# RWKV layer of a two-layer trunk: raw weight loads kept three ahead in another ring, and half of the output weight staged through three tiles

## The chip, the cores and the metric

One core of one Trainium2 chip runs the whole kernel in one launch. The metric is device time in microseconds (us), from a median of separate runs; lower is better. The engines are TensorE (PE for its matmuls, PEld for its weight loads), VectorE (DVE), ScalarE (ACT), GpSimd (POOL) and SyncE (SP), which in this kernel issues all transfers between DRAM and on-chip memory, in one order.

## What is computed

A sequence of 2048 tokens of width 1024 in float32 passes two layers. Each adds to x a normalised mixer of the normalised x. Layer 1 is gated linear attention. Layer 2, which the change touches, is RWKV-7 (cut from the reference):

```python
p = h @ w_in                                   # 2048 x 1024 @ 1024 x 4224
p = p + mu * (token_shift(p) - p)
r, k, v, gate, wd, ad = jnp.split(p, ...)
...
def step(S, inp):                              # over the 2048 tokens, 16 heads of 64
    r_t, w_t, k_t, v_t, kk_t, a_t = inp
    sa = jnp.einsum('bhvk,bhk->bhv', S, -kk_t)
    S = (S * w_t[:, :, None, :] + sa[..., None] * (kk_t * a_t)[:, :, None, :]
         + v_t[..., None] * k_t[:, :, None, :])
    y = jnp.einsum('bhvk,bhk->bhv', S, r_t)
    return S, y
...
return y.astype(h.dtype) @ w_out               # then: x + RMSNorm_post(this)
```

## The kernel before, in words

Layer 1 and its output projection fill the first 880 us or so. Layer 2 is the function `rwkv`. Tokens are cut in four quarters of 512, channels in eight blocks of 128 (two heads). A **step** handles one quarter of one block in chunks of 64 tokens; there are 32 steps of about 42.5 us, then the output projection. A step's own work (`step`) is projections into its tiles, the decay and rate `a` (ACT, L1219 to L1227), products of the form `TD` (POOL, L1233), the chunk matrices (`pA` on PE writes `ps_tp<-ra,bk`, then an elimination on DVE, L1419 and L1422, tiles `pp` and `L`), and the state chain (PE `ps_ch<-ve,BK`, ACT `ve<-ps_ch,cs`, L1601). One of its tiles is `ra`, a 128 x 1024 tile that holds alpha and r, from a ring of three buffers.

All matmuls that carry float32 precision use a high and a low part of each operand: a **block** is one 128-wide slice of a weight against 512 tokens, 8 slices of the inner size by 3 products (high by high, high by low, low by high), 24 matmuls of 128x512. A block needs its 1024 x 128 weight slice, 512 KB, in three tiles: raw (`ws`, ring of one buffer), high `wh` and low `wl` (rings of two).

- `fetch` (L951 to L961) takes the next entry of the list `blocks` and loads its raw slice into `ws` (SP, L960).
- `split` (L963 on) makes high and low. **Quick** blocks do it on ACT (cast, L139) and DVE (subtract, L140), in halves. The others do it on POOL: high in L989, low in L993, and the order in which POOL comes to these is fixed by the table described below.
- `keep` (L976 to L980) writes high and low of a new weight slice to DRAM, so that later quarters read them back (L999) and don't split again. So new slices are split only in the prologue and in steps 0 to 7.
- Then `fetch` is called for the following block.

Quick are the five blocks with step number 0 (`wa`, `kx`, `rx`, `vx`, and `sg`, the gate), and the last 16 blocks, which are the output projection. There the token slice `ys` of 512 KB takes the part of the weight slice.

The order of the list: four blocks of step 0 come ahead of all steps (the prologue; after it, the blocks of the next step are spread through each step as *filler*: 16 pieces, `f0` to `f15`, each a quarter of a block). Near the end eight blocks called `out` compute the product of the first 1024 tokens with the first half of the output weight `wo` (`outfirst`, L372) and write it to DRAM (`raw`). Then `outproj` (L380 to L446) runs: for each of the eight token blocks of half 0 it reads `raw` back into a `vx` tile, computes the product with wo's second half (24 matmuls into `ps_tp`), and finishes the rows (ACT squares L435, DVE L396 and L400, POOL L401, load of x L395, store L402). For each of the eight token blocks of half 1 both halves of wo are used (48 matmuls into `ps_pj` and `ps_tp`).

wo's halves (and the normalised input of later quarters) come in through `eighths` (L169 to L187): eight pieces of 128x512, each loaded into the one-buffer tile `qs` (SP, L177), cast on ACT into `R` (L180), subtracted on DVE (L184); a piece's subtraction calls `more`, which starts the next piece.

Order within an engine: in the steps PE, DVE, ACT and POOL run in an order fixed by a table (`PLACE`: each named event has a due time in steps). SP's order, and that of all engines outside the steps, is made by a scheduler, so the code below says which instructions exist and what they depend on, and the order views further down say where they stand.

Of the kernel before, what the change touches and what calls it, by code (L numbers as in the profile page):

```python
# [17 lines left out]
P = 128  # L18
# [5 lines left out]
TB = 512  # L24
# [26 lines left out]
class Trunk:  # L51
# [3 lines left out]
    def __init__(self, ctx, tc, ins, out):  # L55
# [12 lines left out]
                a=1, kkx=1, sq=1, y=1, AD=1, L=1, Tl=1, TD=1, TT=1, pp=1, wt=1, wa=1, xw=1, xa=1, us=1,   # L68
# [97 lines left out]

        return split

    def eighths(self, src, done, then):  # L169

        hi = self.t("R", NK, TB, dt=F32R)
        lo = self.t("R", NK, TB, dt=F32R)
        done.append((hi, lo))

        def load(k):
            st = self.t("qs", TB)
            self.nc.sync.dma_start(st, src[k * P:(k + 1) * P, :])  # L177

            def high():
                self.nc.scalar.copy(hi[:, k, :], st)  # L180
                self.put("part.low", low)

            def low():
                self.nc.vector.tensor_sub(lo[:, k, :], st, hi[:, k, :].bitcast(F32))  # L184
                then()

            self.put("part.high", high)  # L187
        return [lambda k=k: load(k) for k in range(NK)]
# [731 lines left out]
    def rwkv(self, g, out):  # L920
        nc, i = self.nc, self.i
        w, wo = i["rwkv_w_in"][0], i["rwkv_w_out"][0]
# [3 lines left out]
        hT, W, tiles, parts = [], [], {}, []  # L926

        keys, blocks = [], []
# [10 lines left out]
        for name, m in keys:  # L939
# [3 lines left out]
            blk = off[name] + (steps[m][1] if name != "wa" else 0)  # L943
            blocks.append((w[:, blk * P:(blk + 1) * P], NK, P, m == 0, blk))

        kept = {}
        blocks += [(self.yrows(1, half, j), NK, P, True, None) for half in range(NH) for j in range(8)]

        nxt, ready = SimpleNamespace(), []

        def fetch():  # L951
            nxt.raw = None
            if not blocks:
                return
            src, a, b, quick, blk = blocks.pop(0)
            if blk in kept:
                nxt.raw = None, quick, blk
                return
            st = self.t("ws", 1024)
            nc.sync.dma_start(st.rearrange("p (k c) -> p k c", k=a), src.rearrange("(k p) c -> p k c", p=P))  # L960
            nxt.raw = st, quick, blk  # L961

        def split(name):  # L963

            if nxt.raw is None:
                return
            st, quick, blk = nxt.raw
            pair = []
            ready.append(pair)

            def parts():
                hi, lo = (self.t(t, 1024, dt=F32R) for t in ("wh", "wl"))
                pair.extend(x.rearrange("p (k c) -> p k c", k=NK) for x in (hi, lo))
                return hi, lo

            def keep(hi, lo):  # L976
                if blk is not None:
                    kept[blk] = [self.dr.tile([P, 1024], F32, tag=f"w{j}_{blk}", name=f"w{j}_{blk}", bufs=1) for j in range(2)]
                    for d, x in zip(kept[blk], (hi, lo)):
                        nc.sync.dma_start(d, x.bitcast(F32))  # L980

            def high():
                hi, lo = parts()
                if quick:
                    self.split(st, hi, lo, True)
                    keep(hi, lo)
                    fetch()
                else:
                    nc.gpsimd.tensor_scalar(hi, st, 1.0, 0.0, op0=ALU.mult, op1=ALU.add)  # L989
                    self.put(name + ".low", lambda: low(hi, lo))  # L990

            def low(hi, lo):
                nc.gpsimd.tensor_sub(lo, st, hi.bitcast(F32))  # L993
                keep(hi, lo)
                fetch()

            if st is None:
                for x, d in zip(parts(), kept[blk]):
                    nc.sync.dma_start(x.bitcast(F32), d)  # L999
                fetch()  # L1000
            elif quick:
                high()
            else:
                self.put(name + ".high", high)

        def more():

            if parts and len(blocks) < 25:
                self.put("part", parts.pop(0))

        def take(name="out"):
            split(name)
            if parts and len(blocks) >= 25 and len(blocks) % self.EVERY == 0:
                self.put("part", parts.pop(0))
            return ready.pop(0)

        def stream():
            for name, m in keys:
                if name == "out":
                    yield from self.outfirst(m, take(name), W[0])  # L1020
                    continue
                half, hp, tb = steps[m]
                blk = off[name] + (hp if name != "wa" else 0)
                o = tiles[name, m] = self.t(name, TB)
                then = None
                if name == "wa":
                    res = tiles["x", m] = []
                    then = lambda o=o, res=res: self.lowrank(o, res)
                yield from self.projw(name, hT[m // NHP], take(name), blk, o, then)
                if name == "sg" and (m == 0 or hp == NHP - 1):  # L1030

                    q = m // NHP + 2 if m else 1
                    if q < NH * NTB:
                        parts.extend(self.eighths(self.h2[q], hT, more))
                    else:
                        ch = q - NH * NTB
                        parts.extend(self.eighths(wo[:, ch * TB:(ch + 1) * TB], W, more))
                        more()
            yield from self.outproj(take, W, g, self.x1, out, raw=self.raw)


# [2 lines left out]
        for m, t in enumerate(self.first):  # L1044
            k = slice(2 * m, 2 * m + 2)
# [9 lines left out]
        nc.gpsimd.memset(self.Ti, 0.0)  # L1055
        fetch()
        split("out")
        filler = stream()

        self.load_up(0)  # L1060
# [643 lines left out]
```

## Time and profile before

| | |
|---|---|
| runs of the kernel before | 2526.58, 2529.47 (median), 2530.96 us |
| the profiled execution | 2529.55 us; its span in the trace 2527.5 us |
| mean granted clock of TensorE | 0.988 of full speed |
| PE busy | 95% of the span, 20049 matmuls |
| ACT, DVE, POOL busy | 65%, 63%, 42% |
| DMA | 312.85 MB, 124 GB/s mean over the span |
| quick splits, L139 / L140 | 116 each, mean 608 / 721 ns |

How to read it. The time of the profiled execution is 2 us above its span and 0.08 us above the median of the runs. PE is busy nearly all the time, so what counts are the few places where PE waits or runs at a lower granted clock. In a row of the timeline, the square bracket behind an instruction is the idle time of its engine ahead of it and what ended that. In a row of windows the first number is the window's length, then come busy time and instruction count of PE, PEld, DVE, ACT and POOL, the granted clock (1.00 is full speed, 2.4 GHz; 0.50 is 1.2 GHz), the share of time that the 16 DMA engines were busy, and GB/s.

### The profile page before, as it was taken

To read this page: it belongs to the slowest core of one execution; us is meant where nothing else is said; L and a number is where in the kernel's file an instruction comes from. 1 tells how busy PE (TensorE), PEld (TensorE's weight loads), DVE (VectorE), ACT (ScalarE), POOL (GpSimd) and SP (SyncE) were. 2 spreads that over 40 slices of the span, in tenths; PEclk is the share of its full clock that TensorE was granted. 3 is DMA by queue.
4 is the path that set the end of the run, shared out by engine and by line. 5 is a ranking of instruction groups with operands and counts; after the bars stand their busy time and mean duration, and the time that the engine had idled before them with its cause. 6 is when DMAs were issued, how large, how long until landed. Compare 5 with 4: busy or idle time off the path is not lost.

```text
span 2527.5 us, 53044 instructions
## 1 busy us (share of the span) xinstructions
PE 2413.4 (95%) x20049; PEld 2015.0 (80%) x20049; DVE 1592.1 (63%) x3339; ACT 1645.6 (65%) x3890; POOL 1056.3 (42%) x1557
## 2 busy tenths in 40 slices
PE   7999999999999979999999999999999999999888
PEld 6988888898788857777778788787787878777667
DVE  6544776445643347878777776767677777774332
ACT  6534565444523336877888888788888888877421
POOL 3213422123355536766544443344433434344332
PEclk9999999999999989999999999999999999999999
DMA  4211343112546565444433333333333333323573
GB/s 147 84 51 51 110 124 97 47 51 82 177 141 222 168 207 164 147 145 145 143 112 131 123 118 112 123 123 115 126 109 114 112 122 124 118 76 97 164 222 110
DMA packets 251862, 312.85 MB, mean 124 GB/s; under 512 B 18745, under 2 KB 180184, under 8 KB 251608
## 3 DMA queue, kind: packets, MB, share of 16 engines
q1 hardware_dynamic: 251608, 309.47, 37.3%
q8 instruction: 159, 2.61, 0.4%
q14 instruction: 95, 0.78, 0.1%
HBM read 230.77 MB, written 78.64 MB: 122 GB/s over the span
## 4 chain that ended last, share of the span: by engine, by line
PE 37%; ACT 17%; DVE 4%; issue 3%; DMA 2%; POOL 1%; POOLq 0%; SPq 0%; ACTq 0%; DVEq 0%
PE ps_pj L103 20%; PE ps_tp L103 9%; PE ps_x L103 3%; ACT AD L1377 2%; PE ps_ch L103 2%; ACT ve L1601 2%; PE ps_y L103 1%; ACT ve L1322 1%; ACT ts L836 1%; ACT BK L1394 1%; DMA ws<-ys 1%; PE ps_tp L1561 1%; ACT y L1615 1%; ACT wt L1492 1%; DVE pp L1419 1%
## 5 line engine op out<-in xcount | busy, mean ns | idle before, releaser
L103 PE MATMUL ps_pj<-R,wh 128*128 128x512 f32 x3648 | 1174.6, 403 | 8.0 <-ACT wh L139 3.0
L103 PEld LDWEIGHTS ps_pj<-R,wh 128*128 128x128 f32 x3648 | 657.5, 190 | 136.3 <-ACT wh L139 3.9
L103 PE MATMUL ps_pj<-R,wl 128*128 128x512 f32 x1824 | 720.7, 395 | 11.6 <-POOL wl L993 8.3
L103 PEld LDWEIGHTS ps_pj<-R,wl 128*128 128x128 f32 x1824 | 344.8, 189 | 92.1 <-POOL wl L993 10.4
L1601 ACT ACTIVATE ve<-ps_ch,cs 64x64 f32<-64x64 f32 x448 | 137.3, 307 | 61.5 <-PE ps_ch L103 52.9
L1419 DVE TENSOR_TENSOR pp<-L 128x14 f32<-128x14 f32 (+6 forms) x448 | 168.3, 376 | 10.5
L103 PE MATMUL ps_tp<-R,wh 128*128 128x512 f32 x512 | 160.7, 394 | 13.1 <-ACT R L180 6.6
L139 ACT CAST wh<-ws 128x512 fp32r<-128x512 f32 (+2 forms) x116 | 64.9, 608 | 140.9 <-PE ps_pj L103 68.8
L1422 DVE TENSOR_TENSOR L<-L,pp 128x14 f32<-128x14 f32 (+6 forms) x448 | 136.9, 306 | 12.2
L140 DVE TENSOR_TENSOR wl<-ws,wh 128x512 fp32r<-128x512 f32 (+2 forms) x116 | 79.7, 721 | 91.1 <-ACT wh L139 91.1
L832 POOL TENSOR_SCALAR carr<-ts 128x1 f32<-128x1 f32 x132 | 32.6, 247 | 248.6 <-ACT ts L836 248.5
L1548 POOL TENSOR_SCALAR A<-ra 64x512 f32<-64x512 f32 x128 | 89.8, 701 | 103.6 <-PE ps_x L103 52.4
L308 POOL TENSOR_TENSOR s<-s,cc 128x1 f32<-128x1 f32 (+1 forms) x96 | 58.0, 605 | 170.4 <-DVE s L306 161.8
L103 PEld LDWEIGHTS ps_tp<-R,wh 128*128 128x128 f32 x512 | 96.5, 189 | 36.1 <-ACT wh L139 7.5
L103 PE MATMUL ps_ch<-ve,BK 128*128 128x128 f32 x512 | 109.2, 295 | 7.3 <-ACT ve L1601 7.1
L1377 ACT COPY AD<-A 32x128 f32<-32x128 f32 x256 | 104.9, 410 | 11.3 <-DVE A L1367 8.3
L103 PEld LDWEIGHTS ps_ch<-ve,BK 128*128 128x128 f32 x512 | 87.3, 189 | 29.9 <-ACT ve L1601 10.6
L836 ACT ACTIVATE ts<-ps_pj,prm 128x512 f32<-128x512 f32 x132 | 91.3, 691 | 21.3 <-PE ps_pj L103 12.8
L1367 DVE TENSOR_TENSOR A<-ps_tp,mask 128x512 f32<-128x512 f32 x128 | 82.4, 683 | 34.2 <-PE ps_tp L103 34.2
L103 PE MATMUL ps_tp<-R,wl 128*128 128x512 f32 x256 | 100.8, 394 | 0.0
L1580 DVE TENSOR_TENSOR BK<-ps_tp,BK 128x256 f32<-128x256 f32 x128 | 53.6, 419 | 68.6 <-PE ps_tp L103 68.4
L103 PE MATMUL ps_pj<-wh,R 128*128 128x256 f32 (+1 forms) x500 | 94.7, 287 | 0.0
(354 smaller groups left out, 5489.4 us busy)
## 6 DMA issues: line engine op xcount, KB each, us to landing
wh<-w SPq DMA_DIRECT2D x99, 512.0 KB, 3.3
wl<-w SPq DMA_DIRECT2D x99, 512.0 KB, 4.2
ws<-in_rwkv_w_in_dram SPq DMA_DIRECT2D x33, 512.0 KB, 4.7
w<-wh SPq DMA_DIRECT2D x33, 512.0 KB, 2.6
w<-wl SPq DMA_DIRECT2D x33, 512.0 KB, 3.1
Ti<-in_gla_w_in_dram SPq DMA_DIRECT2D x32, 512.0 KB, 3.9
ws<-in_gla_w_in_dram SPq DMA_DIRECT2D x32, 512.0 KB, 3.8
ws<-ys SPq DMA_DIRECT2D x32, 512.0 KB, 4.0
```

Source lines behind the costliest of these rows:

```text
L103: return self.nc.tensor.matmul(out, lhsT, rhs, start=start, stop=stop)
L139: self.nc.scalar.copy(hi[:, c], src[:, c])
L140: self.nc.vector.tensor_sub(lo[:, c], src[:, c], hi[:, c].bitcast(F32))
L308: nc.gpsimd.tensor_tensor(r[:, 0:w], u[:, 0:w], self.nhalf.broadcast_to([P, w]), op=ALU.pow)
L836: nc.scalar.activation(ts[:, 1:TB + 1], pp, AF.Copy, scale=self.v["mu"][:, blk:blk + 1])
L1367: dve.tensor_mul(T.A[cg][:, :, :, h, :], V(T.pA[cg][h]), V(self.mask.unsqueeze(1).broadcast_to([P, 4, 2 * C])))
L1377: act.copy(T.AD[q, :, :, cg * 4:cg * 4 + 4].rearrange("p t u c -> p c u t"), T.A[cg][q, :, 0, h, 32 * b:32 * b + 32].rearrange("p c (u t) ...
L1419: dve.tensor_mul(T.u, T.M[:, s + 1:16, s:s + 1].broadcast_to([P, m, s]), T.M[:, s:s + 1, 0:s].broadcast_to([P, m, s]))
L1422: dve.tensor_add(T.M[:, s + 1:16, 0:s], T.M[:, s + 1:16, 0:s], T.u)
L1548: pool.tensor_scalar(T.A[cg][H[h], :, :, h, :], T.ra[H[h], cg * 4:cg * 4 + 4, :].rearrange("p c (b t) -> p c b t", b=2), 1.0, 0.0, op0=ALU ...
L1580: dve.tensor_add(o, T.pG[cg][h][:, :, x], o)
L1601: act.activation(o, x, AF.Copy, scale=k)
```

## The change

1. `fetch` now keeps a list of up to three raw loads while the next block is quick, one otherwise. The raw tile of a quick block comes from the ring `ra` (three buffers of the same size, used by the steps for alpha and r), that of any other block from `ws` as before.
2. `fetch` is called ahead of `keep`, so on SP the next raw load may stand ahead of the write of the low part (and of the high part, where the scheduler places it so).
3. wo's second half goes through three tiles, `qs`, `vx`, `vx`, and three pieces are started at once, each of which starts a further one when it is done.

No arithmetic is added or removed. After line 955 the line numbers move by one to three (L989 is L990 in the changed kernel, L993 L994, L999 L1000, L1233 L1236, L1673 L1676).

```diff
-    def eighths(self, src, done, then):
+    def eighths(self, src, done, then, tags=("qs",)):
...
-            st = self.t("qs", TB)
+            st = self.t(tags[k % len(tags)], TB)
...
-        nxt, ready = SimpleNamespace(), []
+        ahead = lambda blk: blk[3]
+        nxt, ready = SimpleNamespace(raw=[]), []
 
         def fetch():
-            nxt.raw = None
-            if not blocks:
+            while blocks and len(nxt.raw) < (3 if ahead(blocks[0]) else 1):
+                src, a, b, quick, blk = blocks[0]
+                if blk in kept:
+                    nxt.raw.append((None, quick, blk))
+                else:
+                    st = self.t("ra" if ahead(blocks[0]) else "ws", 1024)
+                    nc.sync.dma_start(st.rearrange("p (k c) -> p k c", k=a), src.rearrange("(k p) c -> p k c", p=P))
+                    nxt.raw.append((st, quick, blk))
+                blocks.pop(0)
+
+        def split(name):
+
+            if not nxt.raw:
                 return
-            src, a, b, quick, blk = blocks.pop(0)
-            if blk in kept:
-                nxt.raw = None, quick, blk
-                return
-            st = self.t("ws", 1024)
-            nc.sync.dma_start(st.rearrange("p (k c) -> p k c", k=a), src.rearrange("(k p) c -> p k c", p=P))
-            nxt.raw = st, quick, blk
-
-        def split(name):
-
-            if nxt.raw is None:
-                return
-            st, quick, blk = nxt.raw
+            st, quick, blk = nxt.raw.pop(0)
...
                 if quick:
                     self.split(st, hi, lo, True)
+                    fetch()
                     keep(hi, lo)
-                    fetch()
...
                 nc.gpsimd.tensor_sub(lo, st, hi.bitcast(F32))
+                fetch()
                 keep(hi, lo)
-                fetch()
...
-                        parts.extend(self.eighths(wo[:, ch * TB:(ch + 1) * TB], W, more))
-                        more()
+                        tags = ("qs", "vx", "vx") if ch else ("qs",)
+                        parts.extend(self.eighths(wo[:, ch * TB:(ch + 1) * TB], W, more, tags))
+                        for _ in tags:
+                            more()
```

How it moves instructions, at three places.

POOL at the start of layer 2, from the end of the prologue to the first `TD` of step 0. `ts` and `carr` are small carries of the projections, `kkx` belongs to step 0, each pair `wh`, `wl` is the split of one non-quick block (the first is `kx` of step 1, then `rx`, then `vx`). Before:

```order
L839 TENSOR_SCALAR ts_9340<-carr 128x1
L1248 TENSOR_SCALAR kkx_9413<-kx_9259,prm 128x512
L832 TENSOR_SCALAR carr<-ts_9340 128x1
L839 TENSOR_SCALAR ts_9381<-carr 128x1
L989 TENSOR_SCALAR wh_9346<-ws_9313 128x1024
L993 TENSOR_TENSOR wl_9347<-ws_9313,wh_9346 128x1024
L832 TENSOR_SCALAR carr<-ts_9381 128x1
L839 TENSOR_SCALAR ts_9444<-carr 128x1
L989 TENSOR_SCALAR wh_9387<-ws_9354 128x1024
```

and with the change:

```order
L990 TENSOR_SCALAR wh_9346<-ws_9309 128x1024
L994 TENSOR_TENSOR wl_9347<-ws_9309,wh_9346 128x1024
L839 TENSOR_SCALAR ts_9340<-carr 128x1
L1251 TENSOR_SCALAR kkx_9415<-kx_9261,prm 128x512
L832 TENSOR_SCALAR carr<-ts_9340 128x1
L839 TENSOR_SCALAR ts_9381<-carr 128x1
L990 TENSOR_SCALAR wh_9387<-ws_9350 128x1024
L832 TENSOR_SCALAR carr<-ts_9381 128x1
L994 TENSOR_TENSOR wl_9388<-ws_9350,wh_9387 128x1024
L839 TENSOR_SCALAR ts_9446<-carr 128x1
```

The first pair has moved ahead of the carries and of `kkx`; the second and third pair, and `TD` behind them, stand as they did.

SP around the last step, where wo's second half (`in_rwkv_w_out_dram`) and the first token blocks of the output projection (`ys_0_95`) are loaded. Before:

```order
L960 DMA ws_28592<-ys_1_96 128x8x128
L177 DMA qs_28596<-in_rwkv_w_out_dram 128x512
L378 DMA raw<-kx_28618 128x512
L960 DMA ws_28669<-ys_1_96 128x8x128
L177 DMA qs_28648<-in_rwkv_w_out_dram 128x512
L177 DMA qs_28685<-in_rwkv_w_out_dram 128x512
L378 DMA raw<-rx_28701 128x512
L177 DMA qs_28721<-in_rwkv_w_out_dram 128x512
L960 DMA ws_28726<-ys_0_95 128x8x128
L395 DMA kx_28851<-x_0_84 128x512
L177 DMA qs_28746<-in_rwkv_w_out_dram 128x512
```

and with the change:

```order
L960 DMA ra_28744<-ys_0_95 128x8x128
L1676 DMA ys_3_98<-sg_27838 128x512
L960 DMA ws_28596<-ys_1_96 128x8x128
L177 DMA qs_28604<-in_rwkv_w_out_dram 128x512
L177 DMA vx_28606<-in_rwkv_w_out_dram 128x512
L177 DMA vx_28608<-in_rwkv_w_out_dram 128x512
L378 DMA raw<-kx_28630 128x512
L960 DMA ws_28687<-ys_1_96 128x8x128
L177 DMA qs_28664<-in_rwkv_w_out_dram 128x512
L177 DMA vx_28666<-in_rwkv_w_out_dram 128x512
```

The loads of wo come in threes, and the third token block of the output projection (`ra_28744`) is already loaded ahead of them; the first two stand 13 and 8 rows further up.

ACT in the state chain of the last step. Before:

```order
L1601 ACTIVATE S_9160<-ps_ch_28427,cs_27233 64x64 x2
L180 CAST R_28512<-qs_28515 128x512
L1601 ACTIVATE ve_28059<-ps_ch_28585,cs_27803 64x64 x2
L1601 ACTIVATE ve_28059<-ps_ch_28608,cs_27803 64x64 x2
L377 COPY kx_28618<-ps_pj_28514 128x512
L1601 ACTIVATE ve_28059<-ps_ch_28625,cs_27803 64x64 x2
L1601 ACTIVATE ve_28060<-ps_ch_28629,cs_27803 64x64 x2
L180 CAST R_28512<-qs_28596 128x512
```

and with the change:

```order
L1604 ACTIVATE S_9160<-ps_ch_28427,cs_27233 64x64 x2
L180 CAST R_28512<-qs_28515 128x512
L180 CAST R_28512<-vx_28517 128x512
L180 CAST R_28512<-vx_28519 128x512
L1604 ACTIVATE ve_28059<-ps_ch_28589,cs_27803 64x64 x2
L1604 ACTIVATE ve_28059<-ps_ch_28620,cs_27803 64x64 x2
L377 COPY kx_28630<-ps_pj_28514 128x512
L1604 ACTIVATE ve_28059<-ps_ch_28637,cs_27803 64x64 x2
L1604 ACTIVATE ve_28060<-ps_ch_28641,cs_27803 64x64 x2
L180 CAST R_28512<-qs_28604 128x512
L180 CAST R_28512<-vx_28606 128x512
L180 CAST R_28512<-vx_28608 128x512
```

At two places three casts of wo stand where one stood, each time ahead of a `ve` of the chain; the casts that stood further back are gone from there.

## Rows read from the trace of the kernel before

**Rows 1.** Chain of waits that ended last, share of the span by engine.

```profile
PE 37%; ACT 17%; DVE 4%; issue 3%; DMA 2%; POOL 1%; POOLq 0%; SPq 0%; ACTq 0%; DVEq 0%
```

**Rows 2.** Windows: length, five engines' busy us, granted clock, DMA share, GB/s.

```profile
900.63:907.00 6.37, 6.37 (x16) 5.04 (x17) 2.42 (x5) 1.47 (x3) 0.89 (x2) 0.53 0.63 187
1084.60:1136.20 51.60, 46.23 (x444) 37.63 (x443) 40.61 (x71) 37.09 (x88) 32.84 (x41) 0.90 0.44 141
1136.20:1184.40 48.20, 44.54 (x446) 36.66 (x446) 37.59 (x74) 36.02 (x87) 33.08 (x42) 0.93 0.44 143
1273.70:1316.40 42.70, 42.35 (x448) 34.64 (x448) 31.12 (x71) 35.51 (x86) 22.22 (x36) 1.00 0.32 116
2368.80:2432.02 63.22, 48.84 (x194) 36.05 (x192) 25.93 (x48) 21.40 (x52) 22.14 (x21) 0.95 0.70 222
2381.00:2385.00 4.00, 3.87 (x9) 2.84 (x10) 1.09 (x4) 1.51 (x5) 0.55 (x1) 0.55 0.52 162
2400.00:2432.00 32.00, 24.50 (x99) 17.44 (x97) 11.73 (x25) 10.44 (x26) 12.76 (x13) 1.00 0.79 247
2432.00:2519.00 87.00, 86.98 (x384) 71.99 (x384) 23.51 (x48) 18.66 (x47) 24.57 (x24) 1.00 0.45 143
```

**Rows 3.** Timeline of PE, start of layer 2: start, duration, instruction, idle before.

```profile
900.63 0.80 PE L103 MATMUL ps_pj<-R,wl 128*128 128x512 f32 x1 [3.30 <-DVE wl L140]
...
917.56 0.50 PE L103 MATMUL ps_pj<-R,wl 128*128 128x512 f32 x1 [1.71 <-POOL wl L993]
...
941.63 0.76 PE L103 MATMUL ps_tp<-ra,bk 64*128 64x128 f32 x2 [3.17 <-POOL ts L839]
```

**Rows 4.** Timeline of DVE at the same place.

```profile
896.61 3.42 DVE L866 RECIPROCAL wa<-wa 64x64 f32<-64x64 f32 x8
899.96 1.22 DVE L140 TENSOR_TENSOR wl<-ws,wh 128x512 fp32r<-128x512 f32 x2
```

**Rows 5.** Timeline of POOL, from the prologue's end to TD.

```profile
914.01 1.06 POOL L989 TENSOR_SCALAR wh<-ws 128x1024 fp32r<-128x1024 f32 x1 [3.34 <-DMA ws<-in_rwkv_w_in_dram]
...
922.72 1.40 POOL L989 TENSOR_SCALAR wh<-ws 128x1024 fp32r<-128x1024 f32 x1 [4.78 <-DMA ws<-in_rwkv_w_in_dram]
...
932.08 1.30 POOL L989 TENSOR_SCALAR wh<-ws 128x1024 fp32r<-128x1024 f32 x1 [5.27 <-issue]
...
935.78 0.74 POOL L1233 TENSOR_TENSOR TD<-a,s 128x256 f32<-128x256 f32 x1
...
962.79 1.46 POOL L989 TENSOR_SCALAR wh<-ws 128x1024 fp32r<-128x1024 f32 x1 [5.88 <-DMA ws<-in_rwkv_w_in_dram]
```

**Rows 6.** Timeline of ACT: what TD reads.

```profile
924.90 0.61 ACT L1227 ACTIVATE a<-a 128x512 f32<-128x512 f32 x1
```

**Rows 7.** Timelines of DVE and POOL: one elimination subtraction beside a split, and alone.

```profile
1086.56 2.45 DVE L1419 TENSOR_TENSOR pp<-L 128x54 f32<-128x54 f32 x1
1086.55 2.38 POOL L993 TENSOR_TENSOR wl<-ws,wh 128x1024 fp32r<-128x1024 f32 x1
1222.59 0.22 DVE L1419 TENSOR_TENSOR pp<-L 128x54 f32<-128x54 f32 x1
```

**Rows 8.** Timeline of PE in the output projection, half 0.

```profile
2376.24 0.50 PE L103 MATMUL ps_tp<-R,wh 128*128 128x512 f32 x1 [3.20 <-ACT R L180]
...
2381.13 1.52 PE L103 MATMUL ps_tp<-R,wh 128*128 128x512 f32 x2 [3.43 <-ACT R L180]
...
2424.35 0.73 PE L103 MATMUL ps_tp<-R,wh 128*128 128x512 f32 x2 [1.49 <-ACT wh L139]
```

**Rows 9.** Chain of waits in the same stretch: start, duration, what.

```profile
2402.96 5.57 DMA ws<-ys
```

**Rows 10.** DMA view of 2395 to 2435 us: GB/s in 40 slices of 1 us.

```profile
GB/s 244 246 288 233 280 340 330 160 231 251 96 263 379 383 184 176 324 98 120 338 392 371 82 254 281 94 258 336 354 223 152 315 93 101 323 400 191 18 188 305
```

**Rows 11.** Timelines of POOL and SP: last use of an `ra` tile, and SP's next transfer.

```profile
2334.27 1.31 POOL L1548 TENSOR_SCALAR A<-ra 64x512 f32<-64x512 f32 x2 [1.35 <-issue]
2337.63 0.32 SPq L1673 DMA_DIRECT2D ys<-sg  x1
```

## The prediction

> **What bounds the kernel now.** I read the chain of waits first: PE has 37% of it, ACT 17%, DMA only 2% [rows 1]. Then the windows, stage by stage [rows 2]: a normal step is nearly all matmul (42.35 of 42.70 us at granted clock 1.00, the row at 1273.70), and so is half 1 of the output projection (86.98 of 87.00). In such stages an earlier load is worth nothing. From 2432.00 to 2519.00 384 matmuls pass, so a block of 24 costs 87.00 / 384 x 24 = 5.44 us. What can be gained lies where PE falls behind that: the start of layer 2, steps 4 and 5 (51.60 and 48.20 us), and half 0 of the output projection (63.22 us for eight blocks).
>
> **Start of layer 2.** The first loss is the block `rx` of step 0. Its raw slice came late, so its low part stands on DVE behind eight reciprocals of 3.42 us and is made at 899.96 to 901.2 [rows 4]. PE waited 3.30 us for it [rows 3] and then ran at a granted clock of 0.53: 16 matmuls in 6.37 us, where 16 x 0.227 = 3.63 would do [rows 2], 2.7 us more. The second loss lies on POOL. It comes to the splits of three blocks of step 1 in a fixed order, and each waits for the one raw tile: 3.34, 4.78 and 5.27 us [rows 5]. Behind the third stands `TD` at 935.78, though its input `a` was ready at 924.90 + 0.61 = 925.5 [rows 6]. `TD` feeds the chunk matrices, which PE begins at 941.63 [rows 3].
>
> With the change the raw slices of step 0's blocks go to `ra`, so `ws` is free and the raw slice of `kx` of step 1 is on the chip long before. What its split then waits for is a free `wh` (a ring of two): the end of `rx` of step 0 on PE. That block had two matmuls done before the wait and 16 more by 907.00 [rows 2]; the last six take 1.4, so it ends at 908.4, and with the change at 908.4 - 3.3 - 2.7 = 902.4. A split takes 1.06 for the high part [rows 5] and about 2.4 for the low [rows 7]: done by 905.9, against 917.5 now (the wait of PE at 917.56 ends there [rows 3]), 11.6 earlier. The next two links stay bound by the load, as the raw tile of non-quick blocks is still single: high to high 922.72 - 914.01 = 8.7 and 932.08 - 922.72 = 9.4 now [rows 5], less up to 1.2 each, because the next load is issued ahead of the write of the low part. So `TD` comes 11.6 to 14.0 earlier. By then `a` is ready, since it moves up with PE (3.3 + 2.7 + 1.7 = 7.7 earlier, 917.8). I take **-12.5**. Bounds: -6.0, if only the loss at `rx` vanishes; -18, if `TD` followed `a` at once. The steps behind are PE's, so what is won here stays won.
>
> **Steps 1 to 7.** The only edit is the load ahead of the write. The wait at 962.79 is 5.88 us [rows 5]; against 4.78 in the row at 922.72 some 1.1 us can go. I take **-1.5**, this wait and a little of the others. Bounds: the slow steps 4 and 5 have DVE subtractions of the elimination that take 2.45 us beside a POOL split and 0.22 alone [rows 7]. If the splits slid off them, 51.60 + 48.20 - 2 x 42.70 = 14.4 us would come back; if they slid onto them in other steps, as much would be lost (the third rival).
>
> **Output projection, half 0.** Eight blocks should take 8 x 5.44 = 43.5 and take 63.22, so 19.7 are lost. First, wo's second half arrives piece by piece through one tile: PE waits 3.20 and 3.43 us [rows 8], and then 9 matmuls need 3.87 us at a granted clock of 0.55 instead of 2.04 [rows 2]: 8.5 in all. Then the last five blocks each wait for the token slice: load 5.57 [rows 9], a cast of 0.6, the low part, and only then the next load. PE's starts at 2424.35 and 2432.02 are 7.6 apart, with waits of about 1.5 [rows 8]: five times about 2.2 is 10.8. Both causes go. Three token slices are loaded in advance; wo in threes starts far enough ahead.
>
> Two things are given back. DMA: a block moves two token halves, one raw result, two loads of x and two stores, 7 x 262144 B = 1.84 MB. The stretch ran at 247 GB/s with a DMA share of 0.79 [rows 2], so 247 / 0.79 = 313 at full share, 5.9 us per block instead of 5.44: 8 x 0.43 = 3.4 lost. But three token slices (1.57 MB) come in before the stretch, and (8 x 1.84 - 1.57) / 313 = 42 us fits in 43.5, so the loss is between 0 and 3.4; I take 2. The state chain of step 31: two extra casts of 0.6 stand ahead of a `ve` on ACT at two places, and a cast may wait for its piece: I take 1.5, between 0 and 3.4 (one such wait, as in rows 8). Sum **-19.7 + 2 + 1.5 = -16.2**; bounds -19.7 and -2.3 (first rival).
>
> On this stretch a rule can be set against the row: 313 GB/s is inferred from a mean, and single slices of 1 us reach 383 to 400 [rows 10]. The Trainium skill, "DMA: Bandwidth & Descriptors", section "Specifications", gives a limit of about 358 GB/s from device memory to one core; an estimate by it is 5.1 us per block, nothing is given back, and the sum below would be 2497.3. Its figure is exceeded in single slices here, and the mean of the stretch is far below it, so no row here settles it.
>
> SP's order could take the gain away, as one transfer there that waits for a free `ra` holds all behind it. The last use of an `ra` tile ends at 2334.27 + 1.31 = 2335.6, and SP's next transfer comes at 2337.63 [rows 11]: nothing is held, cost 0; if it were, wo would come later and W's waits of 6.6 would return. Half 1 is PE's, cost 0 for its loads.
>
> **Sum.** -12.5 - 1.5 - 16.2 = -30.2 against the profiled execution of 2529.55 us (0.08 over the median of the runs): **2499.3 us**. A measurement of this kernel can tell about 0.2%, 5 us, from no change.
>
> **Rivals.**
> 1. *Half 0 is bound by DMA.* The loads only queue behind one another, and the rate stays at the 247 GB/s that it shows: 1.84 MB / 247 = 7.4 us per block, almost the 7.6 of now. 8 x (7.43 - 5.44) = 15.9 of the 19.7 stay lost, and with the state chain's 1.5 the tail gains 2.3: 2513.2. For it: share 0.79 already. Against it: the present waits are serial, load then split then load. Chance 0.15.
> 2. *The start gives only the loss at `rx`.* Something else holds `TD` or PE where it is: -6.0 instead of -12.5, 2505.8. For it: the links of `rx` and `vx` of step 1 stay load-bound, and PE had 3.17 us of other waits before 941.63. Chance 0.13.
> 3. *Splits collide with the elimination in more steps.* The splits on POOL come earlier or later against DVE by some us. Steps 4 and 5 cost 51.60 - 42.70 = 8.9 and 48.20 - 42.70 = 5.5, mean 7.2 each, with a granted clock of 0.90 and 0.93 [rows 2]. Five more steps with new weights (1, 2, 3, 6, 7) could go the same way: +36, 2535.3, slower. It decides from 30.2 / 7.2, a little over four more slow steps. Against it: the table's order is unchanged, and three steps of the seven would have to move from one side of a 2 us overlap to the other at the least. The Trainium skill, "SBUF — State Buffer", section "Who interferes with whom", says that a DVE instruction with two inputs there and a POOL instruction that reads there shut each other out for a whole instruction; 2.45 beside 0.22 us agrees. Chance 0.04.
> 4. *The slow steps vanish.* The shift takes the splits off the elimination in steps 4 and 5: 14.4 more, 2484.9. Chance 0.06.
> 5. *The change does not act.* SP is held by an `ra` tile at both places, so loads come as late as before: 2529. Chance 0.04.
>
> **How the numbers follow.** The forecast has the remaining 0.58, of which 0.15 is for the case that DMA takes nothing back (2497.3). Range: upwards to rivals 1 and 2 each, with 3.6 us for half of one more slow step, 2517; downwards to the forecast with one slow step relieved (7.2) and the tail's 2 + 1.5 not given back, 2488. Left out are rivals 3, 4, 5 and the far ends, some 2 in 10. Faster by over 0.2%: forecast and rivals 1, 2, 4, 0.92; within 0.2%: rival 5, 0.04; slower: rival 3, 0.04.
>
> **What would show it.** At the start: no wait of 3.30 at `rx`, no drop of the granted clock there, the first non-quick split near 903, and `TD` near 923. In steps: 4 and 5 still long, others near 42.7. In half 0: casts of wo without waits of PE above 1 us, the cast L139 no longer waiting for `ws<-ys`, block starts 5.4 to 5.9 apart, DMA share over 0.85. It is wrong if block starts stay 7 us apart, if `TD` moves by less than 8, or if more steps than two exceed 46 us ahead of step 8.

## The result, and the profile after

The changed kernel takes 2497.81 us (median; 2495.46 to 2500.48), against 2528.02 us for the kernel before: a ratio of 0.9882, 95% interval 0.9867 to 0.9896. That is about 30 us less, clear of the 0.2% that a measurement tells from no change. The forecast was 2499.3 us, with a range of 2488 to 2517. The profiled execution of the changed kernel is the slowest of its four: 2500.48 us, with a span of 2498.4, so 29.1 us less than the span before.

The first view is PE's timeline at the start of layer 2, the rows that answer to [rows 3]:

```profile
900.77 0.73 PE L103 MATMUL ps_pj<-R,wh 128*128 128x512 f32 x2 [0.72 <-DVE kx L829]
920.69 0.50 PE L103 MATMUL ps_pj<-R,wl 128*128 128x512 f32 x1 [0.16 <-POOL wl L994]
926.89 2.96 PE L103 MATMUL ps_tp<-ra,bk 64*128 64x128 f32 x16 [3.60 <-POOL ts L839]
```

The waits of 3.30 for the low part of `rx` and of 1.71 for the low part of the next block are gone, and the chunk matrices begin at 926.89 instead of 941.63. POOL's timeline there, as [rows 5]:

```profile
899.90 1.06 POOL L990 TENSOR_SCALAR wh<-ws 128x1024 fp32r<-128x1024 f32 x1 [3.38 <-PE ps_pj L103]
...
908.42 1.06 POOL L990 TENSOR_SCALAR wh<-ws 128x1024 fp32r<-128x1024 f32 x1 [3.20 <-DMA ws<-in_rwkv_w_in_dram]
...
916.62 1.05 POOL L990 TENSOR_SCALAR wh<-ws 128x1024 fp32r<-128x1024 f32 x1 [2.67 <-PE ps_tp L103]
...
920.60 1.18 POOL L1236 TENSOR_TENSOR TD<-a,s 128x256 f32<-128x256 f32 x1
```

The first split waits no longer for its load but for PE, that is for a free `wh`. The links behind it, from one high part to the next, are 8.5 and 8.2 us, where they were 8.7 and 9.4; the first ends with a load as before, the second with a release by PE. `TD` starts 15.2 us earlier.

The windows of steps 4, 5 and 6 and of half 0 of the output projection (columns as in [rows 2]):

```profile
1067.80:1117.40 49.60, 43.87 (x444) 35.45 (x443) 40.93 (x71) 37.14 (x88) 32.44 (x41) 0.97 0.44 147
1117.40:1165.90 48.50, 44.63 (x444) 36.63 (x444) 38.36 (x72) 35.89 (x86) 33.16 (x41) 0.93 0.43 142
1165.90:1213.90 48.00, 44.89 (x447) 36.84 (x446) 34.97 (x73) 36.07 (x87) 29.96 (x39) 0.93 0.44 147
2357.33:2403.10 45.77, 44.05 (x194) 35.88 (x192) 24.34 (x43) 18.23 (x45) 20.10 (x19) 1.00 0.83 257
```

Steps 4 and 5 are still long, and step 6, which took 42.5 us before, has joined them. Half 0 takes 45.77 us instead of 63.22, at granted clock 1.00. Some of the waits in it (columns: engine, line and what it waited for; sum, times, longest, in us), for the stretch 2340 to 2403:

```profile
ACT kkx L435 <- DMA vx<-raw: 14.0, 3, 5.1
ACT kkx L435 <- PE ps_tp L103: 6.2, 2, 3.1
ACT wh L139 <- PE ps_tp L103: 5.7, 2, 2.9
PE ps_tp L103 <- DVE ts L400: 1.7, 2, 0.9
```

No wait of PE for the token slices or for wo is left. What PE still waits for, 1.7 us, is a free result bank behind DVE's L400, which follows the squares of `raw` on ACT; those wait for the load of `raw`. PE's two waits stand at the start of the seventh and the eighth block:

```profile
2390.97 0.70 PE L103 MATMUL ps_tp<-R,wh 128*128 128x512 f32 x2 [0.84 <-DVE ts L400]
2397.57 0.70 PE L103 MATMUL ps_tp<-R,wh 128*128 128x512 f32 x2 [0.88 <-DVE ts L400]
```

The first five blocks, and then the sixth and the seventh, as windows:

```profile
2357.33:2384.53 27.20, 27.20 (x122) 22.52 (x121) 16.89 (x26) 11.21 (x27) 12.06 (x11) 1.00 0.76 240
2384.53:2390.97 6.44, 5.60 (x26) 4.35 (x24) 2.93 (x6) 2.34 (x6) 2.42 (x3) 1.00 0.94 276
2390.97:2397.57 6.60, 5.72 (x24) 4.42 (x25) 2.93 (x6) 2.34 (x6) 2.53 (x3) 1.00 0.98 307
```

So five blocks pass at 5.44 us each, PE's own pace, and the loss comes behind them, where the DMA engines are busy 94% and 98% of the time.

Where the 29.1 us come from, by the memset that opens each step (POOL, L1163 before, L1166 after) and the starts of the two halves:

| stretch | before | after | difference |
|---|---|---|---|
| up to the opening of step 0 | 891.97 | 890.86 | -1.1 |
| step 0, with the prologue's end | 64.2 | 50.3 | -13.9 |
| steps 1 to 30 | 1303.1 | 1306.0 | +2.9 |
| step 31 to half 0 | 109.5 | 110.2 | +0.7 |
| half 0 | 63.2 | 45.8 | -17.4 |
| half 1 and the end | 95.4 | 95.3 | -0.1 |

The first row differs by as much among kernels that don't differ there (890.0 to 893.7 in the runs below), so it is not put down to the change.

### The profile page after: what moved, and what is told of

The parts are those of the page before. It is cut to its first block, busy times and chain, and to the rows that moved or that the text cites. A ratio compares the mean times of both kernels' runs of the same rounds, so it can differ in the third digit from the quotient of the medians.

```text
span 2498.4 us, 53047 instructions
## 1 busy us (share of the span) xinstructions
PE 2404.0 (96%) x20049; PEld 2011.4 (81%) x20049; DVE 1601.1 (64%) x3339; ACT 1646.3 (66%) x3890; POOL 1065.7 (43%) x1557
## 4 chain that ended last, share of the span: by engine, by line
PE 37%; ACT 18%; DVE 4%; issue 2%; DMA 1%; POOL 1%; POOLq 0%; SPq 0%; ACTq 0%; DVEq 0%
PE ps_pj L103 20%; PE ps_tp L103 9%; PE ps_x L103 3%; ACT AD L1380 2%; PE ps_ch L103 2%; ACT ve L1604 2%; ACT ts L836 1%; ACT ve L1325 1%; PE ps_y L103 1%; ACT BK L1397 1%; ACT y L1618 1%; PE ps_tp L1564 1%; ACT wt L1495 1%; ACT sq L1278 1%; DVE pp L1422 1%
## 5 line engine op out<-in xcount | busy, mean ns | idle before, releaser
L103 PE MATMUL ps_ch<-ve,BK 128*128 128x128 f32 x512 | 109.5, 296 | 7.8 <-ACT ve L1604 7.5
L1583 DVE TENSOR_TENSOR BK<-ps_tp,BK 128x256 f32<-128x256 f32 x128 | 53.7, 419 | 69.6 <-PE ps_tp L103 69.6
L103 PE MATMUL ps_ch<-wh,R 128*128 128x256 f32 (+1 forms) x500 | 94.3, 286 | 0.0
L798 POOL TENSOR_SCALAR y<-BK,cs 128x256 f32<-128x256 f32 x64 | 36.6, 571 | 132.4 <-DVE BK L800 121.3
```

What stands on the lines that cost most here:

```text
L103: return self.nc.tensor.matmul(out, lhsT, rhs, start=start, stop=stop)
L798: nc.gpsimd.tensor_scalar(Qf[:, n % 2, :], Qn, f[:, n:n + 1], 0.0, op0=ALU.mult, op1=ALU.add)
L1583: dve.tensor_add(o, T.pG[cg][h][:, :, x], o)
```

## The experiments

### Which part gives what

Five kernels hold one part or two of the change, a sixth the whole with one edit undone.

`e1_first`: raw slices three ahead for step 0's blocks alone.

```diff
-        ahead = lambda blk: blk[3]
+        ahead = lambda blk: blk[3] and blk[4] is not None
...
-                    fetch()
                     keep(hi, lo)
+                    fetch()
...
-                fetch()
                 keep(hi, lo)
+                fetch()
...
-                        tags = ("qs", "vx", "vx") if ch else ("qs",)
+                        tags = ("qs",)
```

> Only the five quick weight blocks of step 0 are loaded three ahead in the alpha/r ring; the output projection's token slices, the order of load and write, and wo's second half stand as before. Theory (each place gains by itself, and the early raw slices alone make the start faster): about 15 us less than before, TD near 921, half 0 of the output projection unchanged at about 63 us; steps 4 to 6 may differ by a few us either way, since the splits on GpSimd shift against the elimination. Rival (the start is faster because the next load is issued ahead of the write): at most 6 us less, TD later than 928.

Measured: 2512.34 against 2527.53 us, ratio 0.9938 (0.9921 to 0.9955), 15.2 less. Step 0 takes 51.4 us instead of 64.2, half 0 64.8. In the profiled execution steps 4 and 5 are shorter too, 47.2 and 46.9 us instead of 51.6 and 48.1, so not all of the total is the start's. `TD` stands at 923.51, later than expected, because the opening of step 0 was late too (892.3); from there it is 31.2 us away, where it was 43.8 before. So the early raw slices alone give 12.6 of the 14.1 us that the whole change gives on this distance (29.7 us).

`e4_reorder`: the order of load and write alone; all raw slices one at a time in `ws`, wo through one tile.

```diff
-        ahead = lambda blk: blk[3]
+        ahead = lambda blk: False
...
-                        tags = ("qs", "vx", "vx") if ch else ("qs",)
+                        tags = ("qs",)
```

> Only the order: the next raw load is issued ahead of the write of the low part; all raw slices and wo one at a time as before. Theory (the order alone hardly helps the start, and shifts the splits of steps 1 to 7 so that step 6 collides too): TD 1 to 4 us earlier than 935.8, steps 4, 5 and 6 near 49.6, 48.5 and 48.0, output projection as before, in sum 2 us more to 3 us less than before. Rival (the order is what made the whole change's step 1 shorter and its start early): 6 us less or more than that.

Measured: 2524.88 against 2526.26 us, ratio 0.9994 (0.9982 to 1.0005), no difference. The sum was as expected, its parts were not: `TD` comes at 928.32, 7.5 us earlier, and step 0 takes 56.0 us. So the order alone does help the start, by more than the expectation had it; from the opening of step 0 it gives 7.1 us, and beside the early raw slices 1.5 us of that are left (29.7 for 31.2 us in `e1_first` and `e3_noreorder`). In the profiled execution (span 2522.5) 8.1 us won in step 0 leave 5.0: steps 1 to 30 take 2.7 us more, with steps 4, 5 and 6 at 49.6, 48.4 and 48.1, and half 0 1.7 more.

`e3_noreorder`: the whole change, with the two calls in their old order.

```diff
-                    fetch()
                     keep(hi, lo)
+                    fetch()
...
-                fetch()
                 keep(hi, lo)
+                fetch()
```

> The whole change, but the next raw load is again issued after both writes of the high and low parts. Theory (the order of load and write does nothing for the start, and only decides by some tenths of a us where the splits of steps 1 to 7 fall): TD within 2 us of 920.6, half 0 46 us, step 6 back to 42.5 us, so 2 to 8 us less than with the whole change. Rival (the order is a part of the gain): 3 to 8 us more than with the whole change, with TD near 924.

Measured: 2490.92 against 2527.53 us, ratio 0.9855 (0.9841 to 0.9869), some 7 us less than the whole change. `TD` at 921.24, half 0 45.4, step 0 50.6. Windows of steps 4 to 6:

```profile
1068.77:1120.43 51.66, 46.29 (x444) 37.63 (x443) 40.59 (x72) 37.14 (x88) 32.84 (x42) 0.90 0.44 142
1120.43:1168.56 48.13, 44.44 (x446) 36.59 (x445) 37.59 (x74) 35.95 (x87) 32.63 (x41) 0.93 0.44 143
1168.56:1211.04 42.48, 41.55 (x446) 34.29 (x445) 35.48 (x71) 35.94 (x86) 29.81 (x39) 1.00 0.50 161
```

These are the lengths of before to 0.1 us. So the order of load and write costs 5.5 us in step 6, and this holds over the other kernels: without the new order step 6 takes 42.5 to 42.7 us in all seven of them, with it 48.0 and 48.1 where the split is not touched. Step 4 takes 2.0 less with the new order, but the kernels with the old order without a delay take 47.2 to 51.8 us there, so this is not put down to it. Over steps 1 to 30 the whole change takes 3.4 us more than this kernel. The profiled executions of the two are 9.0 us apart, and most of what is left of that lies in step 31: from its opening to half 0 this kernel takes 105.5 us, the whole change 110.2. That part does not follow the order either: `e7_noread` and `f1_later` below have the new order and take 106.5 and 105.2, `e5_tokens` the old one and takes 109.7.

`e2_tail`, `e5_tokens`, `e6_wo`: the output projection's parts. The first has both, the second the token slices three ahead, the third wo in three tiles; the start and the order of the two calls (the diff above) are as before in all three.

```diff
-        ahead = lambda blk: blk[3]
+        ahead = lambda blk: blk[3] and blk[4] is None    # e2_tail, e5_tokens
+        ahead = lambda blk: False                        # e6_wo
...
-                        tags = ("qs", "vx", "vx") if ch else ("qs",)
+                        tags = ("qs",)    # e5_tokens
```

> Only the output projection is changed: its token slices three ahead, wo's second half in three tiles. Theory: the start and all steps as before to 0.3 us, half 0 takes 46 us instead of 63, in sum 17 us less than before. Rival (part of the gain in half 0 comes from the shifted stages ahead of it): 10 us less or fewer.

> Only the output projection's token slices three ahead; wo's second half through one tile and the start as before. Theory (the two losses of half 0 are separate: waits for wo at its first block, and the load of the token slice at the later ones): half 0 falls from 63.2 to 52 to 55 us, the waits of TensorE for wo at its first block stay at 3 us each. Rival (either part alone gives nearly the whole, or nothing, since what is late next takes its place): under 49 or over 60 us.

> Only wo's second half in three tiles; the token slices one ahead as before. Theory (separate losses): half 0 falls from 63.2 by 8 us to about 55 us, with no wait for wo at the first block. Rival (TensorE then only comes earlier to blocks whose token slices are not there, which cost 7.6 us each from the second block on): 5.4 + 7 x 7.6 = 58.6 us or more, a gain of under 5.

Measured:

| kernel | time, us | ratio (interval) | half 0, us |
|---|---|---|---|
| e2_tail | 2506.23 | 0.9919 (0.9907 to 0.9930) | 47.5 |
| e5_tokens | 2518.62 | 0.9957 (0.9940 to 0.9974) | 55.3 |
| e6_wo | 2518.74 | 0.9956 (0.9941 to 0.9971) | 55.8 |

The start stays: step 0 takes 64.5, 63.8 and 66.8 us. The two losses of half 0 are separate: the parts give 7.9 and 7.4 us, both together 15.7. Where the expectation had 46 us for both, it took 47.5. The times of `e5_tokens` and `e6_wo` are 11.8 and 11.7 us below before, more than half 0 gives: steps 1 to 30 are 3.3 us shorter in the first, and step 31 up to half 0 4.0 in the second. PE's rows in half 0 of `e5_tokens`:

```profile
2373.21 0.49 PE L103 MATMUL ps_tp<-R,wh 128*128 128x512 f32 x1 [3.37 <-ACT R L180]
2378.12 1.52 PE L103 MATMUL ps_tp<-R,wh 128*128 128x512 f32 x2 [3.44 <-ACT R L180]
2409.06 0.70 PE L103 MATMUL ps_tp<-R,wh 128*128 128x512 f32 x2 [0.98 <-DVE ts L400]
```

and of `e6_wo`:

```profile
2407.66 0.73 PE L103 MATMUL ps_tp<-R,wh 128*128 128x512 f32 x2 [1.65 <-ACT wh L139]
2415.22 0.73 PE L103 MATMUL ps_tp<-R,wh 128*128 128x512 f32 x2 [1.55 <-ACT wh L139]
2422.83 0.73 PE L103 MATMUL ps_pj<-R,wh 128*128 128x512 f32 x2 [1.58 <-ACT wh L139]
```

With the token slices ahead the two waits for wo stay as in [rows 8]; with wo ahead the waits for token slices stay. Taken over all runs `e2_tail` gains 21.3 us, 4 more than expected; its step 31 is 3.0 us shorter up to half 0 (106.5 against 109.5).

### Why steps 4 to 6 are long

In the changed kernel step 6 shows at its beginning what steps 4 and 5 showed there before. Its rows on DVE, POOL and PE:

```profile
1168.39 2.38 DVE L1422 TENSOR_TENSOR pp<-L 128x56 f32<-128x56 f32 x1
1170.69 0.41 DVE L1583 TENSOR_TENSOR BK<-ps_tp,BK 128x256 f32<-128x256 f32 x1
1167.82 2.87 POOL L994 TENSOR_TENSOR wl<-ws,wh 128x1024 fp32r<-128x1024 f32 x1
1171.58 1.67 PE L103 MATMUL ps_tp<-a,A 64*128 64x128 f32 x8 [2.15 <-DVE A L1583]
```

The split's low part runs beside the elimination, whose subtraction takes 2.38 us instead of 0.2; the additions L1583 behind it are late, PE waits 2.15 us for them, and the step runs at a granted clock of 0.93. In `e3_noreorder` DVE was ahead by a little:

```profile
1169.80 1.05 DVE L1422 TENSOR_TENSOR pp<-L 128x56 f32<-128x56 f32 x1
1170.76 0.41 DVE L1583 TENSOR_TENSOR BK<-ps_tp,BK 128x256 f32<-128x256 f32 x1
1170.86 2.38 POOL L994 TENSOR_TENSOR wl<-ws,wh 128x1024 fp32r<-128x1024 f32 x1
```

There the additions start 0.1 us ahead of the low part, and nothing is lost. By what way the order of two transfers on SP puts DVE 0.5 us further back here is not shown. Two kernels test the collision.

`e7_noread`: in steps 4 to 6 GpSimd fills the low part of the first split with zeros instead (that low part is left out of the products).

```diff
-                nc.gpsimd.tensor_sub(lo, st, hi.bitcast(F32))
+                if name == "kx" and 4 <= (self.clock or 0) < 7:
+                    nc.gpsimd.memset(lo.bitcast(F32), 0.0)
+                else:
+                    nc.gpsimd.tensor_sub(lo, st, hi.bitcast(F32))
```

> The whole change, but in steps 4, 5 and 6 the low part of the step's first split is filled with zeros by GpSimd (an instruction that writes as much and reads nothing), so the low part of three weight slices is left out of the products. Theory (the elimination's instructions on VectorE are shut out by the reading of GpSimd's subtraction): no instruction of the elimination beside the fill takes over 1 us, the waits of TensorE for the additions behind it go, and steps 4 to 6 fall to 42.5 to 44.5 us. Rival (any work of GpSimd in that place, or its writing, holds VectorE up): instructions of 2 us beside the fill, and steps as long as before.

Measured: 2487.67 against 2530.43 us, ratio 0.9832 (0.9817 to 0.9846). POOL's row of the fill and DVE's rows beside it in step 4:

```profile
1070.72 0.95 POOL L995 MEMSET wl<- 128x1024 f32 x1
1070.87 0.21 DVE L1428 TENSOR_TENSOR L<-L,pp 128x50 f32<-128x50 f32 x1
1071.11 0.22 DVE L1425 TENSOR_TENSOR pp<-L 128x54 f32<-128x54 f32 x1
1071.36 0.22 DVE L1428 TENSOR_TENSOR L<-L,pp 128x54 f32<-128x54 f32 x1
```

Three instructions of the elimination pass within the fill at their usual 0.21 to 0.22 us, so a GpSimd instruction that only writes does not hold them up. (The Trainium skill, "SBUF — State Buffer", section "Who interferes with whom", says the same of a VectorE instruction with two inputs: it contends with a GpSimd instruction that reads there, not with one that only writes.) Steps 4, 5 and 6 take 46.9, 43.2 and 42.9 us: 13.2 less than in the changed kernel, though the fill is also shorter than the subtraction (0.95 for 2.4 us), so that some of it would have come with that alone. So this one instruction makes steps 5 and 6 long. In step 4 it is a part only, 2.7 us: another instruction of the same kind lies 25 us into that step (L1333 on DVE takes 2.88 us beside a split), and behind it PE waits 2.14 us for `TD`. There the expectation was wrong. This second collision stands in the kernel before too, with a wait of 2.16 us.

`f1_later`: the whole change, in steps 4 to 6 the same low part put some us later.

```diff
-                    self.put(name + ".low", lambda: low(hi, lo))
+                    late = 0.2 if name == "kx" and 4 <= (self.clock or 0) < 7 else 0.0
+                    self.put(name + ".low", lambda: low(hi, lo), (self.clock or 0) + late)
```

> The whole change, and in steps 4, 5 and 6 the low part of the step's first split (GpSimd, 2.4 us) is put behind the split of the up-projection, some 10 us later in the step; its block is used about 19 us into the step. Theory (these steps are long because this one instruction shuts out the elimination's instructions on VectorE, the additions behind them are late, TensorE waits 2 to 3 us and then runs at half its granted clock): all three fall from 49.6, 48.5 and 48.0 to 42.5 to 43.5 us, in sum 15 to 18 us less than the whole change. Rival (they are long for another reason, as the DMA traffic of new weights or the clock alone): no difference over 5 us.

Measured: 2492.08 against 2527.53 us, ratio 0.9861 (0.9848 to 0.9873), near 6 us less than the whole change. Windows of steps 4 to 6, and a row of DVE and of PE in step 6:

```profile
1073.03:1120.53 47.50, 42.71 (x445) 34.27 (x444) 42.63 (x73) 37.21 (x89) 32.47 (x42) 1.00 0.45 154
1120.53:1165.11 44.58, 42.06 (x444) 34.26 (x444) 40.21 (x71) 35.82 (x87) 31.69 (x42) 1.00 0.46 155
1165.11:1209.39 44.28, 42.13 (x446) 34.45 (x446) 36.74 (x72) 36.00 (x87) 28.90 (x39) 1.00 0.48 159
```

```profile
1172.96 2.34 DVE L1426 TENSOR_TENSOR L<-L,pp 128x50 f32<-128x50 f32 x1
1178.37 0.49 PE L103 MATMUL ps_ch<-ve,BK 128*128 128x128 f32 x2 [1.17 <-ACT ve L1605]
```

The three steps give 9.8 us together, not 15 to 18. The wait for the additions is gone and the granted clock is 1.00 throughout, but POOL came to the moved instruction at 7.7 to 8.5 us into the step, earlier than assumed, when the elimination still ran; it shuts out another of its instructions, and PE has a wait of 1.17 in the state chain. Steps 1 and 2, in which nothing was moved, took 3.3 us more than in the changed kernel, which the run leaves unexplained.

`f2_both`: `e3_noreorder` with that delay in steps 4 and 5.

> The whole change with the next load issued after both writes, and in steps 4 and 5 the low part of the first split some us later in the step. Theory: step 6 stays at 42.5 as without the delay, steps 4 and 5 fall from 51.7 and 48.1 to about 47.5 and 44.6 (what the delay gave with the other order), so 7 to 8 us less than without the delay. Rival (the two do not add up, since one edit moves the splits that the other has placed): within 3 us of the faster of the two.

Measured: 2487.87 against 2530.43 us, ratio 0.9833 (0.9819 to 0.9848), the fastest of the kernels that compute everything, and about 0.5% under the changed kernel (0.9882). Steps 4, 5 and 6 take 47.8, 44.7 and 42.5 us, 7.2 us less than in `e3_noreorder`: the two edits add up in these steps. By the ratios (0.9833 and 0.9855) some 5 us of that are left, at the edge of what can be told.

## Why the prediction was right

The two large mechanisms stood as forecast, at the start and in half 0, and the sum is right to 1.1 us in the traces (-29.1 for -30.2), though its terms erred by more, in opposite senses.

- **Start: -12.5 forecast, -13.9 in step 0.** The first split waits for PE's release of `wh`, as argued, from 899.90 where 902.4 was worked out; the links behind it are 8.5 and 8.2 (forecast 7.5 to 8.7, and 8.2 to 9.4), though the second was ended by PE and not by a load; `TD` at 920.60 (923). Rival 2 is excluded. `e1_first` shows that the raw slices in the other ring alone give most of it, 12.6 of 14.1 us.
- **Steps 1 to 7: -1.5 forecast, +2.2 measured (+2.9 over steps 1 to 30), and here the working failed.** The step that failed is "the only edit is the load ahead of the write": a term was made of a wait that gets shorter, while the same edit decides on which side of DVE's additions a split's low part comes. The wait of 5.88 us did shrink, to 3.93 (6.08 in `e3_noreorder`). Steps 1 and 4 gained 1.8 and 2.0, step 5 lost 0.4 and step 6 5.5. Rival 3 was this mechanism, right in place and nearly in price (5.5 for 7.2), but it struck one step more and not five. `e3_noreorder` and `e4_reorder` show that the order of load and write is its cause: without it step 6 takes 42.5, with it alone 48.1.
- **Half 0: -19.7 + 2 = -17.7 forecast, -17.4 measured.** Both parts were needed: the token slices alone give 7.9 and wo alone 7.4 (forecast 10.8, from starts that lie 7.67 us apart and not 7.6, and 8.5). What is given back, 2.3 us, is near the 2 taken. It lies in two blocks alone, whose starts are followed by the next after 6.44 and 6.60 us, where a block at full DMA share was put at 5.9; all earlier ones take 5.44. The DMA share over the half is 0.83, under the 0.85 that was named as a sign, but in these two blocks 0.94 and 0.98. So the price comes late, as it would once the slices loaded ahead are used up, which fits the term. The wait seen there is ACT's for the load of `raw`; whether that load is late because the DMA engines are full, or because it stands behind other transfers in SP's order, no run separates. Rival 1, with 7.4 us for every block, did not come about. The Trainium skill, "DMA: Bandwidth & Descriptors", section "Specifications", gives a limit of about 358 GB/s from device memory to one core. The two blocks moved 276 and 307 GB/s, below it; by the prediction's estimate from that limit nothing would have been given back, and 2.3 us were.
- **State chain: 1.5 forecast, 0.44 us found.** PE has one further wait in it, the first of these rows of the changed kernel:

```profile
2336.99 0.49 PE L103 MATMUL ps_ch<-ve,BK 128*128 128x128 f32 x2 [0.44 <-ACT ve L1604]
2338.20 0.49 PE L103 MATMUL ps_ch<-ve,BK 128*128 128x128 f32 x2 [0.72 <-ACT ve L1604]
```

The second stands in the kernel before as well:

```profile
2351.30 0.49 PE L103 MATMUL ps_ch<-ve,BK 128*128 128x128 f32 x2 [0.72 <-ACT ve L1601]
```

A wait of 0.44 or 0.45 us is there in all seven kernels that load wo in threes, and in none of the other four.

- **Rival 4** did not come about, **rival 5** neither. SP did wait for a free `ra` tile, 2.1 and 7.1 us between the opening of step 31 and half 0, where the working had "nothing is held". It cost nothing: the transfer behind each, a store of `ys`, had to wait 1.6 us longer for its own data.

That the total fell so near the forecast is thus partly luck: the start gave 1.4 more than forecast, the stretch ahead of it 1.1 that the change does not explain, the chain cost less, and the steps gave 4.4 less.

## What to carry to other kernels

Where a block waits for load, split and load in turn, more raw buffers can be worth most of the serial part, and a ring that is idle at that time will do; cost it by the waits on the path, and look for what stands in order behind them on the engine that splits (here POOL's `TD`, which gave more than PE's own wait). An edit that only changes the order in which two transfers are issued is not free when two engines shut each other out near that place: find the pairs of long instructions in the trace, look how far from the edge each step lies, and give the sign of such a term as open. When a change has several parts, run each alone; here the others gave 37 us together, and with the one that looked harmless 30 were left. Then look where in the traces such a difference lies: of the 9 us between the two, some 3 are steps that this edit lengthens, and 5 a collision in step 31 that does not follow it.

## What the runs showed of the hardware

A subtraction on GpSimd over 128x1024 elements (2.4 us) and a small one on VectorE that runs 0.2 us alone end together: in steps 1 to 6 of all kernels the small one ends within 0.1 us of the large one, and takes 2.34 to 2.47 us where both begin within 0.15 us. A fill that only writes as many elements does not do this (`e7_noread`). The price is not the 2.2 us. It can be less: steps 1 to 3 of the changed kernel each hold such a pair (2.46, 2.46 and 1.85 us for the small one) and take 40.4, 43.5 and 42.9 us. And it can be more, where PE waits for what comes next on VectorE. In step 6 of the changed kernel PE waits 2.15 us behind it and then runs at a granted clock of 0.54 for over 7 us:

```profile
1171.58:1179.00 7.42, 7.36 (x29) 5.98 (x30) 5.40 (x17) 1.10 (x3) 0.92 (x2) 0.54 0.45 144
```

The step loses 5.5 us. In `f1_later`, with a wait of 1.17 us, the granted clock stays at 1.00 and step 6 loses 1.8. But the length of the wait does not settle what the clock does. The second collision of step 4 makes PE wait 2.16 us both in the kernel before and in `f1_later`; before, the granted clock is 0.55 behind it, in `f1_later` 1.00. The row of PE and the window from there on, before and then in `f1_later`:

```profile
1118.46 1.08 PE L103 MATMUL ps_x<-TD,A 32*32 32x32 f32 x64 [2.16 <-DVE TD L1440]
1118.46:1122.00 3.54, 3.54 (x124) 3.25 (x127) 2.04 (x5) 2.23 (x5) 1.82 (x4) 0.55 0.86 228
```

```profile
1103.61 0.75 PE L103 MATMUL ps_x<-TD,A 32*32 32x32 f32 x64 [2.16 <-DVE TD L1444]
1103.61:1108.00 4.39, 4.39 (x152) 3.81 (x152) 3.80 (x8) 3.54 (x9) 1.82 (x4) 1.00 0.82 267
```

What decides it is not shown. It also makes the 2.0 us by which step 4 of the changed kernel is shorter than before: both have the two waits, 2.88 and 2.17 us after and 2.72 and 2.16 before, at a granted clock of 0.97 and 0.90 over the step.

The same collision as in step 6 stands at the opening of step 31 in five kernels: before, `e1_first`, `e4_reorder`, `e5_tokens` and the changed one. PE waits 2.17 to 2.79 us there, and the stretch to half 0 takes 108.7 to 110.2 us. In the other six PE waits 0.65 to 0.86 us, and the stretch takes 105.2 to 106.5. Neither the order of load and write nor the early raw slices divide the two groups. All six short ones load wo in threes and four of the five long ones don't; the changed kernel is the exception, so why it collides there stays open. Runs of one kernel spread by 5 us or more (2495.46 to 2500.48 for the changed one, 2503.86 to 2520.30 for `e1_first`), which would fit collisions that come and go from run to run; there is one profile of each kernel, so this stays open too.
